# Copies inside SBUF of the keys' and the queries' parts issued from GpSimd's queue instead of SyncE's, in a one-core S5 and sliding-window attention layer

## The chip, the cores and the metric

The kernel runs on one core of a Trainium2 chip. The metric is the device time of one execution in microseconds (us), from the program's start on the core to its end. The engines are named as the profile names them: TensorE (PE, with its weight loads as PEld), VectorE (DVE), ScalarE (ACT), GpSimd (POOL) and SyncE (SP). A DMA is issued by an instruction on the queue of one of SyncE, ScalarE and GpSimd, and that queue is worked off in order.

## What is computed

One layer on x of 1024 tokens by 1024 features, in float32: a projection into six parts, an S5 state-space branch over `u`, sliding-window attention of 8 query heads on 2 key heads over blocks of 128 tokens, both gated by a SiLU, an output projection, and a gate with a per-layer embedding. Cut to what matters here:

```python
hn = rms_norm(h, pre_norm_g[i])
u_ssm, z_ssm, q, k, v, z_attn = jnp.split(hn @ w_in[i], SPLIT_IDX, axis=-1)
ssm_out = s5_branch(u_ssm, ...) * jax.nn.silu(z_ssm)      # scan, gelu, then a Glu with w_glu
attn_out = swa_branch(q, k, v, attn_sinks[i]) * jax.nn.silu(z_attn)
mixed = jnp.concatenate([ssm_out, attn_out], axis=-1) @ w_out[i]
h = h + rms_norm(mixed, post_norm_g[i])
gate = jax.nn.sigmoid(h @ pl_w_gate[i] + pl_b_gate[i])
h = h + gate * (p[i] @ pl_w_proj[i])

# in swa_branch, for each block of 128 queries and the two blocks of keys that it sees:
scores = jnp.einsum('bnqkgd,bnskd->bnkgqs', qb, kb) * scale   # plus ALiBi bias, masked
m = jnp.maximum(jnp.max(scores, axis=-1, keepdims=True), sink)
e = jnp.exp(scores - m)
probs = e / (jnp.sum(e, axis=-1, keepdims=True) + jnp.exp(sink - m))
```

## The kernel before

**Large matmuls.** Each float32 operand is split into a high part and a remainder (`split_to`: ScalarE rounds to the high part on L88, VectorE subtracts on L89), and `product` makes three matmuls of each: high by high (L116), remainder by high (L118), high by remainder (L120). The weights come in parts of 256 KB: `load_part` loads one into `w_st` (L94, on SyncE's queue) and splits it into `w_hi` and `w_lo`. There are two `w_st`, so a load must wait until both parts of the one before last are made, and four of each `w_hi` and `w_lo`.

**State-space branch.** It runs in eight batches of four channel groups. `into_states` of a batch loads `U` and `coef` (L500), builds `mt`, which TensorE transposes (L515), forms the batch's inputs (`w`), and stores a small table `t7` to DRAM (L537) and reads it back in another layout as `tz` (L539); `phases` makes `co` and `si` on VectorE; `scan` runs the recurrence (L579) and swaps halves by two DMAs (L568, L569); `outputs` multiplies with `tz` and `qt` into `ps_y` (L592, L594), applies the gelu on ScalarE (L596, with a load of its function table) and stores `y` to DRAM (L599).

**Projections between the batches.** `project_k` stands ahead of the batches. The list `tiles` (values, four tiles of queries, four of `z_attn`, two of `z_ssm`) is dealt out over the batches, so that TensorE has these matmuls to do while VectorE works on the scan. The code of a batch has a raised priority.

**Keys.** `project_k` scales the keys into `k_f` (128 rows: two key heads of 64 features) and splits them into `k_hi` and `k_lo`. For the scores each head's 64 rows must stand in both halves of the partitions: eight DMAs of 64 rows by 1024 float32 (256 KB each) copy `k_hi` and `k_lo` into `kk` (L616, L617).

**Queries and attention.** `queries(b)` splits a block's 128 queries into `bq_hi` and `bq_lo`, of which there is one buffer each, and four DMAs of 64 by 512 float32 (128 KB each) put the high part of a key head's queries and their remainder into the two halves of `bq` (L710, L711). A unit is half a block (four heads), sixteen in all, whose steps are interleaved with other work: `scores` (GpSimd copies the sink into `sc`, L731; TensorE multiplies `bq` with `kk`, L737 and L738; in block 0 ScalarE copies the scores to `sc`, L740), `maxima` (GpSimd masks in block 0, L748; VectorE, L754), exponents on ScalarE (L761), the reciprocal (L766) and the normalisation on ScalarE or VectorE (L769, L771), transposes (L776), the copy to `p` (L778), values (L794).

**Glu.** It loads `w_glu` (L858) and, for a chunk of channels, the batches' `y` from DRAM into `y_all` (L886), multiplies them in float32 (L866) and gates with a tanh (L869). Its first tiles run between the first units of the attention. The output projection and the tail with the per-layer embedding follow.

**What sets the order.** The program's text gives priorities; a scheduler with a simulated timeline then orders the instructions of each engine's queue, DMA issues among them, and puts in the waits. So an edit in one place can move instructions on any engine after it.

Of the kernel before, what the change touches and what calls it, by code (L numbers as in the profile page):

```python
# [11 lines left out]
F32 = mybir.dt.float32  # L12
# [41 lines left out]
def layer_kernel(  # L54
# [3 lines left out]
    nc = tc.nc  # L58
    V, S, Q, PE = nc.vector, nc.scalar, nc.gpsimd, nc.tensor

    with ExitStack() as top:
# [16 lines left out]
        def t4(shape, dt, name):  # L78
            return mp.tile(shape, dt, name=name, tag="t4", bufs=BUFS["t4"])

        def t2(shape, dt, name, tag):
            return mp.tile(shape, dt, name=name, tag=tag, bufs=BUFS[tag])
# [4 lines left out]
        def split_to(hi, lo, t):  # L87
            S.activation(hi, t, AF.Copy)  # L88
            V.tensor_tensor(out=lo, in0=t, in1=hi.bitcast(F32), op=ALU.subtract)  # L89
# [82 lines left out]
        def place(k):  # L172
            return (x_st if k < 4 else x_sq)[:, k % 4, :]
# [97 lines left out]
        def project(m):  # L271
            w = load_split(w_in[m], KT)
            ps = psum_pair()
            product(ps, w, xact, [(k, k) for k in range(KT)])
            return ps
# [190 lines left out]
        with tc.issue_after(loaded.ins):  # L466
            nc.sync.dma_start(out=t7_dr[:, :, :, 0:CH, :].rearrange("c g q k n -> (g q) c (k n)"),
                                in_=zero.unsqueeze(1).broadcast_to([GB * PC, G // GB, CH * PC]))
# [78 lines left out]
        def phases(b):  # L547
            gs = slice(b["c"] * GB, (b["c"] + 1) * GB)
            co, si = b["co"], b["si"] = big("co", "co"), big("si", "si")

            def a_(t):
                return t[:, gs, :].unsqueeze(3).broadcast_to([P, GB, 8, 16])

            def b_(t):
                return t[:, gs, :].unsqueeze(2).broadcast_to([P, GB, 8, 16])

            a = big("t3", "ta")
            tt(ev(a), a_(e1[1]), b_(e0[1]), ALU.mult)
            tt(ev(co), a_(e1[0]), b_(e0[0]), ALU.mult)
            tt(co, co, a, ALU.subtract)  # L560
            a = big("t4", "ta")
            tt(ev(a), a_(e1[0]), b_(e0[1]), ALU.mult)
            tt(ev(si), a_(e1[1]), b_(e0[0]), ALU.mult)
            tt(si, si, a, ALU.add)
# [7 lines left out]
        def scan(b):  # L572
            w, w2, co, si, c = (b[n] for n in ("w", "w2", "co", "si", "c"))
            tt(w2, w2, si, ALU.mult)
            tt(w, w, co, ALU.mult)
            tt(w, w, w2, ALU.add)
            s = b["s"] = big("s", "w")
            for g in range(GB):
                V.tensor_tensor_scan(out=s[:, g * NC : (g + 1) * NC],  # L579
                                     data0=r8[:, c * GB + g : c * GB + g + 1].broadcast_to([P, NC]),  # L580
                                     data1=w[:, g * NC : (g + 1) * NC], initial=0.0, op0=ALU.mult, op1=ALU.add)
            b["s2"] = swapped(s, nc.sync)

        def outputs(b):
            s, s2, co, si, c, U, tz, qt = (b[n] for n in ("s", "s2", "co", "si", "c", "U", "tz", "qt"))
            tt(s2, s2, si, ALU.mult)
            tt(s, s, co, ALU.mult)
            tt(s, s, s2, ALU.subtract)
            y = t2([P, GB, NC], F32, "y", "sw")
            ps = bank("y")  # L590
            for g in range(GB):
                PE.matmul(ps[:, g * NC : (g + 1) * NC], lhsT=tz[:, g * P : (g + 1) * P], rhs=U[:, g, :],  # L592
                          start=True, stop=False)
                PE.matmul(ps[:, g * NC + 1 : (g + 1) * NC], lhsT=qt[:, g * P : (g + 1) * P],  # L594
                          rhs=s[:, g * NC : (g + 1) * NC - 1], start=False, stop=True)
            S.activation(y, ps.rearrange("p (g c) -> p g c", c=NC), AF.Gelu_apprx_tanh)  # L596
            for g in range(GB):
                r = (c % 2) * 64 + g * PC
                nc.sync.dma_start(out=y_dr[c // 2][r : r + PC].rearrange("q i c -> i q c"), in_=y[:, g, :])  # L599


        def scaled(ps, t, scale=1.0):
            for h, o in enumerate(ps):
                hs = slice(h * HALF, (h + 1) * HALF)
                V.scalar_tensor_tensor(out=t[:, hs], in0=o, scalar=scale, in1=rstd[:, hs], op0=ALU.mult, op1=ALU.mult)
            return t

        def project_k():
            t = scaled(project(8), t4([P, T], F32, "k_f"))
            lo = t4([P, T], F32R, "k_lo")  # L610
            hi = t4([P, T], F32R, "k_hi")
            split_to(hi, lo, t)
            for kv in range(2):
                for half in range(2):
                    rows = slice(64 * half, 64 * half + 64)
                    nc.sync.dma_start(out=kk_hi[rows, kv, :].bitcast(F32), in_=hi[64 * kv : 64 * kv + 64].bitcast(F32))  # L616
                    nc.sync.dma_start(out=kk_lo[rows, kv, :].bitcast(F32), in_=lo[64 * kv : 64 * kv + 64].bitcast(F32))  # L617

        def project_v():
            vt = scaled(project(9), t4([P, T], F32, "v_f"))  # L620
# [33 lines left out]
        kk_hi, kk_lo = kk[:, 0], kk[:, 1]  # L654
# [8 lines left out]
        with tc.high_priority(offset=AHEAD):  # L663
            into_states(batch[0])
            phases(batch[0])
        project_k()
        tiles = ([project_v] + [partial(project_q, m) for m in range(4)] + [partial(project_z_attn, m) for m in range(4)]
                 + [partial(project_z_ssm, m) for m in range(2)])
        for c, b in enumerate(batch):
            with tc.high_priority(offset=AHEAD):  # L670
                scan(b)
                if c + 1 < len(batch):
                    phases(batch[c + 1])
                outputs(b)
                if c + 1 < len(batch):
                    into_states(batch[c + 1])
            for f in tiles[len(tiles) * c // len(batch) : len(tiles) * (c + 1) // len(batch)]:
                f()

# [19 lines left out]
        def queries(b):  # L701

            qs = slice(b * P, (b + 1) * P)
            hi = t2([P, 4, P], F32R, "bq_hi", "mt")
            lo = t2([P, 4, P], F32R, "bq_lo", "m")
            split_to(hi, lo, q_f[:, :, qs])
            st = [t2([P, 4, P], F32R, "bq", t) for t in ("u", "si")]
            for kv in range(2):
                rows, other = slice(64 * kv, 64 * kv + 64), slice(64 - 64 * kv, 128 - 64 * kv)
                nc.sync.dma_start(out=st[kv][rows].bitcast(F32), in_=hi[rows].bitcast(F32))  # L710
                nc.sync.dma_start(out=st[kv][other].bitcast(F32), in_=lo[rows].bitcast(F32))  # L711
            return st

        def stat(name):
# [224 lines left out]
        run_pieces(n, ahead)  # L939
        n = ahead  # L940
        bq = {0: queries(0)}
        for t in range(4 * len(units) + steps[0][1]):
            for step, lag in steps:
# [187 lines left out]
```

## Time and profile before

| | |
|---|---|
| median of 3 runs | 534.99 us (534.62 to 535.94) |
| the profiled execution | 535.14 us |
| its span in the trace | 533.4 us |
| TensorE busy | 97% of the span |
| VectorE | 71% |
| ScalarE | 40% |
| GpSimd | 2% |
| granted TensorE clock, mean | 0.992 of full speed |
| chain that ended last | PE 80%, DVE 9%, DMA 7%, SyncE's queue 1% |

The profiled execution is 0.15 us above the median of the runs, and its span is 1.74 us shorter than its own time, which holds what lies around the program. "Busy" counts instructions and not issues of DMAs. The chain is followed back from the last instruction to what released it; a share of it is what a faster step could at most give.

### The profile page before, as it was taken

To read this page: it belongs to the slowest core of one execution; us is meant where nothing else is said; L and a number is where in the kernel's file an instruction comes from. 1 tells how busy PE (TensorE), PEld (TensorE's weight loads), DVE (VectorE), ACT (ScalarE), POOL (GpSimd) and SP (SyncE) were. 2 spreads that over 40 slices of the span, in tenths; PEclk is the share of its full clock that TensorE was granted. 3 is DMA by queue.
4 is the path that set the end of the run, shared out by engine and by line. 5 is a ranking of instruction groups with operands and counts; after the bars stand their busy time and mean duration, and the time that the engine had idled before them with its cause. 6 is when DMAs were issued, how large, how long until landed. Compare 5 with 4: busy or idle time off the path is not lost.

```text
span 533.4 us, 7319 instructions
## 1 busy us (share of the span) xinstructions
PE 517.3 (97%) x2472; PEld 410.4 (77%) x2472; DVE 379.8 (71%) x864; ACT 214.2 (40%) x443; POOL 8.6 (2%) x37
## 2 busy tenths in 40 slices
PE   7999999999999999999899999999999998999996
PEld 5888887888888888886445767777788886888886
DVE  4778997989889898654699667666467679736232
ACT  5676120311122322233775656667332373223121
POOL 1000000000000000010000000000000000000000
PEclk9999999899999999999999999999999989999999
DMA  7961638344443434559575122101111165124112
GB/s 268 372 233 60 217 93 196 95 128 121 122 117 97 120 95 117 176 145 252 169 213 190 47 60 60 30 22 39 61 49 30 67 218 174 65 80 172 66 39 79
DMA packets 48053, 66.10 MB, mean 124 GB/s; under 512 B 10128, under 2 KB 25232, under 8 KB 48016
## 3 DMA queue, kind: packets, MB, share of 16 engines
q1 hardware_dynamic: 46736, 63.54, 38.6%
q10 hardware_dynamic: 1280, 2.10, 1.5%
q8 instruction: 19, 0.31, 0.3%
q14 instruction: 18, 0.15, 0.1%
HBM read 44.12 MB, written 11.01 MB: 103 GB/s over the span
## 4 chain that ended last, share of the span: by engine, by line
PE 80%; DVE 9%; DMA 7%; SPq 1%; issue 1%; ACT 1%; ACTq 0%; DVEq 0%
PE ps_mm L118 18%; PE ps_mm L116 18%; PE ps_mm L120 18%; PE ps_tab L120 4%; PE ps_tab L116 4%; PE ps_tab L118 4%; PE ps_mm L866 3%; DMA y_all<-y_dr 2%; PE ps_w L794 2%; PE ps_y L794 2%; PE ps_tab L737 1%; PE ps_tab L738 1%; PE ps_y L594 1%; PE ps_w L520 1%; DVE e L314 1%
## 5 line engine op out<-in xcount | busy, mean ns | idle before, releaser
L88 ACT ACTIVATE w_hi<-w_st 128x512 fp32r<-128x512 f32 (+1 forms) x68 | 41.2, 606 | 132.3 <-PE ps_mm L118 80.6
L116 PE MATMUL ps_mm<-x_hi,w_hi 128*128 128x512 f32 x272 | 86.3, 399 | 2.3 <-ACT x_hi L178 1.7
L118 PE MATMUL ps_mm<-x_lo,w_hi 128*128 128x512 f32 x272 | 87.7, 399 | 0.0
L120 PE MATMUL ps_mm<-x_hi,w_lo 128*128 128x512 f32 x272 | 87.4, 398 | 0.0
L89 DVE TENSOR_TENSOR w_lo<-w_st,w_hi 128x512 fp32r<-128x512 f32 (+1 forms) x68 | 44.8, 659 | 38.7 <-ACT w_hi L88 32.4
L116 PEld LDWEIGHTS ps_mm<-x_hi,w_hi 128*128 128x128 f32 x272 | 51.3, 191 | 13.6 <-ACT x_hi L178 2.2
L118 PEld LDWEIGHTS ps_mm<-x_lo,w_hi 128*128 128x128 f32 x272 | 51.6, 191 | 10.5
L120 PEld LDWEIGHTS ps_mm<-x_hi,w_lo 128*128 128x128 f32 x272 | 51.2, 191 | 10.2 <-DVE w_lo L89 0.3
L118 PE MATMUL ps_mm<-h_lo,w_hi 128*128 128x512 f32 (+1 forms) x96 | 30.8, 380 | 0.0
L116 PE MATMUL ps_mm<-h_hi,w_hi 128*128 128x512 f32 (+1 forms) x96 | 30.8, 380 | 0.0
L120 PE MATMUL ps_mm<-h_hi,w_lo 128*128 128x512 f32 (+1 forms) x96 | 30.7, 380 | 0.0
L761 ACT ACTIVATE sc<-sc,mx 128x129 f32<-128x129 f32 x64 | 25.1, 395 | 12.9 <-DVE mx L754 12.7
L866 PE MATMUL ps_mm<-y_all,w_glu 128*128 128x512 f32 x64 | 29.1, 596 | 1.2 <-DMA w_glu<-in_w_glu 1.2
L1028 DVE SCALAR_TENSOR_TENSOR o_t<-o_t,pls 128x512 f32<-128x512 f32 (+1 forms) x17 | 10.9, 658 | 20.0 <-ACT o_t L1027 20.0
L866 PEld LDWEIGHTS ps_mm<-y_all,w_glu 128*128 128x128 f32 x64 | 11.5, 190 | 13.5 <-issue 10.6
L116 PE MATMUL ps_mm<-m_hi,w_hi 128*128 128x512 f32 x64 | 21.8, 404 | 0.0
L120 PE MATMUL ps_mm<-m_hi,w_lo 128*128 128x512 f32 x64 | 21.7, 402 | 0.0
L118 PE MATMUL ps_mm<-m_lo,w_hi 128*128 128x512 f32 x64 | 21.7, 398 | 0.0
L118 PEld LDWEIGHTS ps_mm<-h_lo,w_hi 128*128 128x128 f32 x96 | 18.0, 188 | 3.5
L116 PEld LDWEIGHTS ps_mm<-h_hi,w_hi 128*128 128x128 f32 x96 | 18.0, 188 | 3.5
L120 PEld LDWEIGHTS ps_mm<-h_hi,w_lo 128*128 128x128 f32 x96 | 18.0, 188 | 3.5
L314 DVE TENSOR_TENSOR sw<-sw,si 128x512 f32<-128x512 f32 x16 | 11.1, 693 | 11.4 <-DMA sw<-s 8.4
(265 smaller groups left out, 1022.9 us busy)
## 6 DMA issues: line engine op xcount, KB each, us to landing
w_st<-in_w_in SPq DMA_DIRECT2D x30, 256.0 KB
w_st<-in_w_out SPq DMA_DIRECT2D x16, 256.0 KB
w_st<-in_w_gate SPq DMA_DIRECT2D x16, 256.0 KB
x<-in_xT SPq DMA_DIRECT2D x8, 512.0 KB
out_T<-o_t SPq DMA_DIRECT2D x15, 256.0 KB
x_sq<-in_xT SPq DMA_DIRECT2D x4, 512.0 KB
x_st<-in_x SPq DMA_DIRECT2D x4, 512.0 KB
x_sq<-in_x SPq DMA_DIRECT2D x4, 512.0 KB
```

What stands on the lines that cost most here:

```text
L88: S.activation(hi, t, AF.Copy)
L89: V.tensor_tensor(out=lo, in0=t, in1=hi.bitcast(F32), op=ALU.subtract)
L116: PE.matmul(o, lhsT=wh, rhs=ah(ka, h), start=f, stop=False)
L118: PE.matmul(o, lhsT=wh, rhs=al(ka, h), start=False, stop=False)
L120: PE.matmul(o, lhsT=wl, rhs=ah(ka, h), start=False, stop=l)
L314: V.tensor_tensor(out=o, in0=a, in1=b, op=op)
L520: PE.matmul(ps[:, g * NC : (g + 1) * NC], lhsT=m[:, g * P : (g + 1) * P], rhs=U[:, g, :], start=True, stop=True)
L594: PE.matmul(ps[:, g * NC + 1 : (g + 1) * NC], lhsT=qt[:, g * P : (g + 1) * P], rhs=s[:, g * NC : (g + 1) * NC - 1], start=False, stop=True)
L761: S.activation(self.sc[:, m, :], self.sc[:, m, :], AF.Exp, bias=self.mx[:, m : m + 1], scale=-1.0, accum_out=self.sm[:, m : m + 1])
L794: PE.matmul(pv[64 * kv : 64 * kv + 64], lhsT=v[:, cols], rhs=p[:, 2 * kv : 2 * kv + 2, :], start=n == 0, stop=n == len(parts) - 1)
L866: PE.matmul(self.ps, lhsT=self.w[:, k, :], rhs=glu_in["y"][:, self.hf, k, :], start=k == 0, stop=k == 3)
L1028: V.scalar_tensor_tensor(out=t, in0=t, scalar=1.0, in1=pls[2 * m + h][:, a : a + n], op0=ALU.add, op1=ALU.mult)
```

## The change

The eight copies of the keys and the four per block of the queries are issued by `nc.gpsimd` instead of `nc.sync`. `project_k` no longer issues the keys' copies itself: it returns four functions, of two copies each, and the loop over the batches calls one of them at the end of each of the first four batches. Line numbers behind it grow by two (the queries' copies are L712 and L713 now, the keys' L615 and L616).

```diff
             split_to(hi, lo, t)
-            for kv in range(2):
-                for half in range(2):
-                    rows = slice(64 * half, 64 * half + 64)
-                    nc.sync.dma_start(out=kk_hi[rows, kv, :].bitcast(F32), in_=hi[64 * kv : 64 * kv + 64].bitcast(F32))
-                    nc.sync.dma_start(out=kk_lo[rows, kv, :].bitcast(F32), in_=lo[64 * kv : 64 * kv + 64].bitcast(F32))
+            def place(kv, half):
+                rows = slice(64 * half, 64 * half + 64)
+                nc.gpsimd.dma_start(out=kk_hi[rows, kv, :].bitcast(F32), in_=hi[64 * kv : 64 * kv + 64].bitcast(F32))
+                nc.gpsimd.dma_start(out=kk_lo[rows, kv, :].bitcast(F32), in_=lo[64 * kv : 64 * kv + 64].bitcast(F32))
+            return [partial(place, kv, half) for kv in range(2) for half in range(2)]
...
-        project_k()
+        placed = project_k()
...
             for f in tiles[len(tiles) * c // len(batch) : len(tiles) * (c + 1) // len(batch)]:
                 f()
+            if placed:
+                placed.pop(0)()
...
             for kv in range(2):
                 rows, other = slice(64 * kv, 64 * kv + 64), slice(64 - 64 * kv, 128 - 64 * kv)
-                nc.sync.dma_start(out=st[kv][rows].bitcast(F32), in_=hi[rows].bitcast(F32))
-                nc.sync.dma_start(out=st[kv][other].bitcast(F32), in_=lo[rows].bitcast(F32))
+                nc.gpsimd.dma_start(out=st[kv][rows].bitcast(F32), in_=hi[rows].bitcast(F32))
+                nc.gpsimd.dma_start(out=st[kv][other].bitcast(F32), in_=lo[rows].bitcast(F32))
             return st
```

SyncE's queue around the keys, before (`t_dr` is the table `t7` in DRAM, `w_st` the staged weights of the next projection):

```order
L94 DMA w_st<-in_w_in 128x512 x2
L537 DMA t_dr<-t_713 16x8x16 x4
L539 DMA tz<-t_dr 128x1x128 x4
L616 DMA kk<-k_hi 64x1024
L617 DMA kk<-k_lo 64x1024
```

Three more pairs like the last two follow, and then `coef` and the weights. The same place now:

```order
L94 DMA w_st<-in_w_in 128x512 x2
L537 DMA t_dr<-t_713 16x8x16 x4
L539 DMA tz<-t_dr 128x1x128 x4
L500 DMA coef<-in_bc 128x256
L94 DMA w_st<-in_w_in 128x512 x3
L568 DMA sw<-s 64x512
L569 DMA sw<-s 64x512
```

The eight rows of the keys are gone, and `coef` and three loads of weights stand right behind `tz`.

GpSimd's queue from the keys to the first unit of the attention, now; before, it held the same rows without the DMAs:

```order
L701 AFFINE_SELECT own_t<-own_t 128x128
L615 DMA kk<-k_hi 64x1024 x4
L616 DMA kk<-k_lo 64x1024 x4
L689 IOTA dist 128x128
L690 IOTA near 128x128
L712 DMA bq<-bq_hi 64x512
L713 DMA bq<-bq_lo 64x512
L712 DMA bq<-bq_hi 64x512
L713 DMA bq<-bq_lo 64x512
L733 COPY sc<-sink 128x4
L750 AFFINE_SELECT sc<-sc 128x4x128
```

All eight copies of the keys stand in one piece, behind masks made at the start (`own_t`); the queries' copies stand ahead of the units' copies of the sink.

ScalarE's queue between the exponents of the first unit and the second block's queries, before:

```order
L761 ACT_TABLE_LOAD
L761 ACTIVATE sc,sm<-sc,mx 128x129 x4
L88 ACTIVATE bq_hi<-q_f 128x512
L596 ACT_TABLE_LOAD
L596 ACTIVATE y<-ps_y 128x512
L740 COPY sc<-ps_tab 128x2x128 x2
L778 COPY p<-ps_w 128x512
L839 ACTIVATE z_tanh<-z_half 128x1024
```

and now:

```order
L763 ACT_TABLE_LOAD
L763 ACTIVATE sc,sm<-sc,mx 128x129 x4
L596 ACT_TABLE_LOAD
L596 ACTIVATE y<-ps_y 128x512
L742 COPY sc<-ps_tab 128x2x128 x2
L780 COPY p<-ps_w 128x512
L88 ACTIVATE bq_hi<-q_f 128x512
L841 ACTIVATE z_tanh<-z_half 128x1024
```

`bq_hi` has moved behind the gelu `y` of the last batch, the scores' copies and `p`.

## Rows read from the trace of the kernel before

**Rows 1.** The page, busy time of each engine: us, share of the span, instructions.

```profile
PE 517.3 (97%) x2472; PEld 410.4 (77%) x2472; DVE 379.8 (71%) x864; ACT 214.2 (40%) x443; POOL 8.6 (2%) x37
```

**Rows 2.** Waits of TensorE, whole span: what waited, for what, us in total, times, longest us.

```profile
PE ps_tab L515 <- DVE mt L314: 1.7, 1, 1.7
...
PE ps_y L776 <- ACT sc L769: 1.4, 1, 1.4
PE ps_mm L866 <- DMA w_glu<-in_w_glu: 1.2, 2, 0.7
...
PE ps_tab L737 <- ACT sc L740: 1.1, 1, 1.1
```

**Rows 3.** Stretches: us, busy PE, PEld, DVE, ACT, POOL, clock, DMA share, GB/s.

```profile
82.00:84.00 2.00, 2.00 (x10) 1.66 (x9) 2.00 (x5) 0.00 (x0) 0.00 (x0) 1.00 1.01 205
...
94.00:96.00 2.00, 1.96 (x14) 1.89 (x15) 2.00 (x6) 0.59 (x1) 0.00 (x0) 0.80 0.36 131
96.00:98.00 2.00, 2.00 (x6) 1.61 (x5) 2.00 (x4) 0.00 (x0) 0.00 (x0) 0.50 0.56 131
98.00:100.00 2.00, 2.00 (x9) 1.56 (x9) 2.00 (x5) 0.00 (x0) 0.00 (x0) 0.84 0.02 3
246.00:248.00 2.00, 2.00 (x10) 1.39 (x9) 0.00 (x0) 0.00 (x0) 0.54 (x3) 1.00 1.05 213
```

**Rows 4.** The chain of waits through 74 to 96 us: start us, us, what.

```profile
87.98 3.88 DMA w_st<-in_w_in
...
91.94 0.64 ACT w_hi L88
```

**Rows 5.** VectorE's timeline: start us, us, instruction, count, [idle before it <- its end].

```profile
80.07 0.73 DVE L89 TENSOR_TENSOR w_lo<-w_st,w_hi 128x512 fp32r<-128x512 f32 x1
...
92.60 0.69 DVE L89 TENSOR_TENSOR w_lo<-w_st,w_hi 128x512 fp32r<-128x512 f32 x1 [3.38 <-ACT w_hi L88]
```

**Rows 6.** SyncE's timeline, 74 to 94 us, issues of DMAs.

```profile
74.87 3.17 SPq L539 DMA_DIRECT2D tz<-t_dr  x4
78.09 0.60 SPq L616 DMA_DIRECT2D kk<-k_hi  x1
...
85.43 1.21 SPq L617 DMA_DIRECT2D kk<-k_lo  x1
86.75 1.13 SPq L500 DMA_DIRECT2D coef<-in_bc  x1
87.98 5.67 SPq L94 DMA_DIRECT2D w_st<-in_w_in  x3
```

**Rows 7.** ScalarE's timeline, 241 to 262 us.

```profile
250.50 0.63 ACT L88 ACTIVATE bq_hi<-q_f 128x512 fp32r<-128x512 f32 x1 [9.05 <-DMA bq<-bq_hi]
...
252.44 0.60 ACT L596 ACTIVATE y<-ps_y 128x512 f32<-128x512 f32 x1
```

**Rows 8.** SyncE's timeline, 236 to 270 us.

```profile
241.98 0.47 SPq L710 DMA_DIRECT2D bq<-bq_hi  x1
...
245.00 2.32 SPq L886 DMA_DIRECT2D y_all<-y_dr  x3
```

**Rows 9.** The chain of waits through 238 to 272 us.

```profile
239.95 5.72 DMA y_all<-y_dr
...
256.57 2.35 DMA bq<-bq_lo
```

**Rows 10.** TensorE's timeline: the first use of `tz`, the last matmul of a batch.

```profile
77.68 0.39 PE L592 MATMUL ps_y<-U,tz 128*128 128x128 f32 x2
...
245.61 0.39 PE L594 MATMUL ps_y<-s,qt 128*128 128x127 f32 x2
```

**Rows 11.** The tile `kk`, its first matmuls: ns min, median, max; first and last start.

```profile
L737 PE MATMUL ps_tab<-kk,bq x64: 222/281/682, 234.8 to 355.6; 128*128 128x256 f32 x56, 128*128 128x128 f32 x8
```

**Rows 12.** A stretch, columns as in rows 3.

```profile
280.00:420.00 140.00, 140.00 (x679) 104.02 (x678) 91.80 (x244) 75.57 (x208) 2.03 (x9) 1.00 0.19 57
```

**Rows 13.** GpSimd's groups of instructions: count, busy us, mean ns, idle before and releasers.

```profile
L731 POOL COPY sc<-sink 128x4 f32<-128x4 f32 x16 | 4.8, 300 | 121.6 <-PE ps_y L776 42.7 <-DVE s L579 30.3 <-PE ps_w L776 30.2
```

## The prediction

> **What bounds the kernel now.** The page comes first. TensorE is busy 517.3 us of the 533.4 us span [rows 1], so a change that touches no matmul can win only where TensorE stands idle or runs at its lower clock, at most 16 us and a little. The wait table of TensorE then says where that is [rows 2]; the reader is to see that four of its waits have to do with work beside which the changed copies stand: 1.7 us before the transposes of `mt`, 1.1 and 1.4 us behind ScalarE's `sc`, and 1.2 us for `w_glu`. They lie in two places.
>
> *Place 1, 92 to 99 us.* TensorE waits 1.7 us for VectorE's `mt`. Behind that wait the granted clock drops: 0.80, 0.50 and 0.84 of full speed in three stretches of 2 us [rows 3]; 0.50 is the 1.2 GHz level. The missing share is (0.20 + 0.50 + 0.16) x 2 us = 1.72 us. The chain of waits [rows 4] says why `mt` is late: VectorE stood idle 3.38 us ahead of a `w_lo` [rows 5], which waited for ScalarE's `w_hi`, which waited for a weight load of 3.88 us that SyncE issued only at 87.98. SyncE's own rows [rows 6] show what it did before: behind the copies of `tz` it issued the eight copies of the keys, from 78.09 to 86.64, and then `coef` and the weights. A timeline lists no semaphore for the weight load, but its buffer is free when VectorE's `w_lo` at 80.07 has read it, by 80.80 [rows 5]. So it was late only because it stood in line behind the keys.
>
> *Place 2, 246 to 270 us.* ScalarE idled 9.05 us before `bq_hi` at 250.50, and that wait names the copies of `bq` as its end [rows 7]: `bq_hi` has one buffer, and the copies that read it had to finish. Those copies were issued at 241.98 and later between two groups of `y_all` loads [rows 8], one of which took 5.72 us, while a later copy of `bq` took 2.35 us [rows 9]. The gelu `y` of the next batch stands behind `bq_hi` on ScalarE and came at 252.44 [rows 7], though its last matmul began at 245.61 [rows 10]. The scores' `sc` copies, the storing of `y` and the third load of `y_all` follow from it. TensorE's idle time here sums to 1.1 + 1.4 + 1.2 = 3.7 us [rows 2].
>
> **The change, part by part.** The keys' eight copies leave SyncE's queue. By the order they are not spread: nothing ahead of the eight on GpSimd's queue has to wait for anything late, so they go out one after another as soon as `k_hi` and `k_lo` exist. The keys are first read at 234.8 us [rows 11], so how long they take costs nothing in itself.
>
> 1. *Weights of place 1.* Without the 8.55 us of issuing, `coef` and the weights follow `tz` at 78.04; the buffer lets the weights go at 80.8, 7.2 us earlier. VectorE comes to its `w_lo` at 92.60 - 3.38 = 89.22. Even a load of 5.72 us, the longest in these rows, ends at 86.5. VectorE's 3.38 us and TensorE's 1.7 us of idle time go: **-1.7 us**. With no idle time ahead of it the clock has no cause to fall: **-1.72 us**; it was at 1.00 in the stretches before [rows 3].
>
> 2. *Keys against `tz`.* Now the copies of the keys run from some 73 us on and meet the storing of `t7` and the load of `tz`, which had the DMA engines nearly to themselves. TensorE reads the first `tz` at 77.68 without having waited [rows 10], and that `tz` was issued at 74.87 [rows 6], so its latency may be at most 2.81 us. An uncontended copy took 2.35 us, a load on full engines 5.72 us [rows 9]. The cost lies between 0 and 5.72 - 2.81 = 2.9 us; I take **+0.9 us**, near the lower third, since the keys' first copies start only as `t7` is stored, and the engines' share is at 1.01 from 82 to 84 us, when five or six of them were issued [rows 3].
>
> 3. *Queries in place 2.* In the new order ScalarE does the gelu `y`, the `sc` copies and `p` ahead of `bq_hi`, and the copies of `bq` neither wait behind the `y_all` loads on SyncE nor delay them. `y` can then go at about 246.1 instead of 252.44. What is late next is not that: the third tile of `w_glu` still stands behind six `y_all` loads, and the engines were at 1.05 of their share from 246 to 248 [rows 3]. Bounds: nothing gained (0), all of it gained (-3.7). I leave a wait of 1.3 us for `w_glu` and `y_all`, about what `w_glu` costs today, and take **-2.3 us**.
>
> 4. *Queries in the attention blocks.* From 280 to 420 us TensorE is busy 140.00 of 140.00 us [rows 12], so there is nothing to gain. GpSimd gets four copies per block, in order with its copies of `sc`, of 0.30 us each [rows 13]. No row shows a copy issued from GpSimd; issues on SyncE held it 0.47 us (`bq`) to 1.21 us (a copy of the keys) [rows 6, 8], and I take 1.1 us, near the dearer of the two, since no row excludes more; what more would cost is rival D. A block takes (355.6 - 234.8) / 7.5 = 16.1 us [rows 11] and GpSimd would be busy 4 x 1.1 + 2 x 0.3 = 5 us of it: **0**. Its cover is those 11 us.
>
> 5. *SyncE without the 32 issues of `bq`*, of some 0.5 us: outside the two places the path doesn't go through it, since TensorE doesn't wait there: 0.
>
> The sum is -1.7 - 1.72 + 0.9 - 2.3 = -4.82 us. The profiled execution took 535.14 us, 0.15 above the median of the runs, so the forecast is 535.14 - 4.82 = 530.32, **530.3 us**. Its own range goes from 535.14 - 1.7 - 1.72 - 3.7 = 528.0 (all of place 2, nothing for `tz`) to 535.14 - 1.7 - 1.72 + 0.9 = 532.6 us (place 1 alone). Smaller than 0.3% (1.6 us) a difference from the median can't be told from none.
>
> **The rivals.**
>
> *A. Place 2 is bound by the transfers, not by the queue.* The engines stand at 1.05 of their share at its start [rows 3]; moving an issue from one queue to another moves no byte less. For it: the two `y_all` loads are what the chain goes through. Against it: ScalarE's 9.05 us is a wait for an order of work, and that order changes. Then only place 1 is won: 535.14 - 3.42 + 0.9 = 532.6 us. The Trainium skill ("DMA: Bandwidth & Descriptors", "Issuing engines are not separate DMA queues") says just this, that DMAs from any engine run on the same 16 engines and a second issuer saves only the sequencer's time. The trace agrees for place 1, where it is the sequencer's 8.55 us that go, and leaves place 2 open. Chance 0.14.
>
> *B. The keys take the engines from `tz`*, and TensorE waits the full 2.9 us at 77.68, after which its clock falls as it did behind 1.7 us in place 1 (another 1.72 us). Place 1 is given back: -3.42 + 2.9 + 1.72 = +1.2, and place 2 stands: 535.14 + 1.2 - 2.3 = 534.0 us. Against it: half of the keys' copies need `k_lo`, which VectorE makes after `k_hi`, and a few us of overlap must more than double a latency. Chance 0.08.
>
> *C. GpSimd can't issue while VectorE works.* VectorE is busy 2.00 of every 2.00 us in place 1's run-up [rows 3]. If GpSimd were shut out, the keys would wait till VectorE idles and only then go; they are not needed for 140 us, `tz` is not disturbed (+0), place 1 is still won. The copies of `bq` would each lose some us, which takes place 2's gain: 535.14 - 3.42 = 531.7 us. The Trainium skill ("SBUF — State Buffer", "SBUF: two separate sides") tells of such a shut-out: a copy issued from GpSimd that takes some 620 ns alone took 3100 ns beside a VectorE copy in its two-port mode. No run here shows it yet; the same page's "Who interferes with whom" holds two-input operations, which fill VectorE here, to bother only GpSimd's reads. Chance 0.08.
>
> *D. GpSimd's queue becomes the bound of the attention (slower).* Its queue is in order, and its `sc` copies stand behind the copies of `bq`; VectorE's maxima and all that follows wait for `sc`. The point from which it decides: a copy of `bq` holds GpSimd over (16.1 - 0.6) / 4 = 3.9 us, by its issue or by waiting for `bq_hi`'s buffer. At 4.5 us a block grows by 2.5 us, and seven blocks by 17: 530.3 + 17 = 547 us. For it: GpSimd does 4.8 us of such `sc` copies in the whole kernel [rows 13] and issues nothing, so no row shows that it can keep up, and each copy waits for its buffers in line. Against it: the issues of SyncE are a quarter as long. Chance 0.14.
>
> **The change does not do what it says:** "spread over later tiles" does not hold in the order (all eight stand together). It costs nothing where the keys are concerned, since the queue that mattered was SyncE's; it is the cause of term 2.
>
> **How the numbers follow.** Forecast 0.56, A 0.14, B 0.08, C 0.08, D 0.14. The range is 527.9 to 534.3: it takes the forecast's own, A, B and C, and leaves out D and the tails. Faster by over 0.3% (below 533.4): forecast, C and nearly all of A, 0.56 + 0.08 + 0.12 = 0.76. Within: B and the rest of A, 0.10. Slower: D, 0.14.
>
> **What would show it.** In the profile after: SyncE issues the weights near 80.8 us right behind `coef`; no idle time ahead of the transposes of `mt`; granted clock 1.00 between 92 and 100 us. If TensorE waits at its first `tz`, term 2 is right in kind, and its length is the price. In place 2 ScalarE's `y` comes before `bq_hi`, near 246 us, and the wait for `bq` is gone; the remaining waits of TensorE there sum to about 1.3 us. GpSimd's rows give the price of an issue, 1.1 us by me; VectorE waiting for GpSimd's `sc` in every block would be D. I am wrong if TensorE's total idle time falls by less than 1.5 us, or if a new wait of over 1 us appears anywhere outside the two places.

## The result, and the profile after

The change makes the kernel slower: 544.20 us median of 5 runs (543.45 to 545.11) against 535.94 (534.62 to 536.54), a ratio of 1.0147 with an interval of 1.0120 to 1.0174. The forecast was 530.3 us with a range up to 534.3.

The page after, busy time, and then the waits of TensorE over the whole span:

```profile
PE 520.3 (96%) x2472; PEld 411.4 (76%) x2472; DVE 379.6 (70%) x864; ACT 214.0 (39%) x443; POOL 29.3 (5%) x77
```

```profile
PE ps_y L592 <- DMA tz<-t_dr: 7.5, 1, 7.5
PE ps_tab L116 <- ACT w L88: 2.1, 1, 2.1
...
PE ps_mm L868 <- DMA w_glu<-in_w_glu: 1.6, 1, 1.6
PE ps_mm L116 <- ACT a_hi L88: 1.2, 1, 1.2
```

Of the four waits of [rows 2] three are gone (for `mt`, and both behind `sc`), and the one for `w_glu` is 1.6 us. In their place stands one of 7.5 us, for `tz`. It is the rival B of the prediction, much larger than it was priced. GpSimd's timeline, SyncE's, and the chain of waits show how it came about:

```profile
72.09 2.19 POOL L615 DMA_DIRECT2D kk<-k_hi  x4 [69.40 <-ACT k_hi L88]
74.27 2.02 POOL L616 DMA_DIRECT2D kk<-k_lo  x4
```

```profile
71.97 4.10 SPq L537 DMA_DIRECT2D t_dr<-t  x4
76.11 7.41 SPq L539 DMA_DIRECT2D tz<-t_dr  x4
83.62 0.54 SPq L500 DMA_DIRECT2D coef<-in_bc  x1
84.58 11.80 SPq L94 DMA_DIRECT2D w_st<-in_w_in  x3
```

```profile
74.33 1.74 SPq L537
...
76.11 9.07 DMA tz<-t_dr
...
85.23 0.79 PE ps_y L592 x2
```

GpSimd issued all eight copies, 2.1 MB, in 4.2 us. SyncE had needed 8.55 us for them [rows 6]. The storing of `t7` and the load of `tz` were issued into the same stretch. SyncE's four issues of `tz` took 7.41 us, where they had taken 3.17 [rows 6]; the first `tz` took 9.07 us, where it had taken 2.81 at most, and landed at 85.18. Stretches of 2 us (columns as in rows 3) show full DMA engines, TensorE without work, and the lower clock behind the wait:

```profile
72.00:74.00 2.00, 2.00 (x13) 1.70 (x12) 2.00 (x6) 0.00 (x0) 1.91 (x4) 1.00 0.60 172
...
76.00:78.00 2.00, 1.73 (x8) 1.11 (x6) 2.00 (x5) 0.08 (x1) 0.29 (x1) 1.00 1.03 264
78.00:80.00 2.00, 0.00 (x0) 0.00 (x0) 1.08 (x2) 0.00 (x0) 0.00 (x0) 1.00 1.00 276
...
86.00:88.00 2.00, 2.00 (x7) 1.52 (x6) 1.19 (x3) 0.63 (x1) 0.00 (x0) 0.50 0.47 129
88.00:90.00 2.00, 2.00 (x6) 1.60 (x5) 2.00 (x4) 0.00 (x0) 0.00 (x0) 0.50 0.00 0
```

A measure of place 1 that all kernels share is the time from TensorE's first forming of batch inputs (L520) to its second. Before:

```profile
71.76 1.05 PE L520 MATMUL ps_w<-U,m 128*128 128x128 f32 x8
...
101.10 1.05 PE L520 MATMUL ps_w<-U,m 128*128 128x128 f32 x8
```

and after:

```profile
71.43 1.05 PE L520 MATMUL ps_w<-U,m 128*128 128x128 f32 x8
...
107.86 1.05 PE L520 MATMUL ps_w<-U,m 128*128 128x128 f32 x8
```

That is 29.34 us before and 36.43 us after, so +7.1 us, most of the 8.3 us between the medians. The spans of the two profiles differ by 9.4 us (533.4 and 542.8). Besides these 7.1 us, 2.7 lie behind the last such forming: from there to the end it takes 322.1 us before and 324.8 after.

A second loss is seen only in the groups of instructions. TensorE's matmuls of the values, in the kernel before (columns: line, operation, shapes, count, busy us, mean ns, idle before) and after:

```profile
L794 PE MATMUL ps_w<-p_own,v_step 128*64 128x256 f32 x28 | 7.5, 392 | 0.0
L794 PE MATMUL ps_y<-p,v_f 128*64 128x256 f32 x32 | 6.5, 405 | 0.0
L794 PE MATMUL ps_w<-p,v_f 128*64 128x256 f32 x32 | 5.2, 404 | 0.0
L794 PE MATMUL ps_y<-p_own,v_step 128*64 128x256 f32 x28 | 5.0, 386 | 0.0
```

```profile
L796 PE MATMUL ps_w<-p_own,v_step 128*64 128x256 f32 x28 | 7.6, 395 | 0.0
L796 PE MATMUL ps_y<-p,v_f 128*64 128x256 f32 x32 | 6.5, 405 | 0.0
L796 PE MATMUL ps_w<-p,v_f 128*64 128x256 f32 x32 | 6.5, 404 | 0.0
L796 PE MATMUL ps_y<-p_own,v_step 128*64 128x256 f32 x28 | 6.3, 390 | 0.0
```

The same 120 records, of nearly the same length each, fill 26.9 us of TensorE's time instead of 24.2. (One matmul of the program is two records here, so these are 60 matmuls.)

### The profile page after: what moved, and what is told of

It reads as the page before. It is cut to its first block, busy times and chain, and to the rows that moved or that the text cites. A ratio compares the mean times of both kernels' runs of the same rounds, so it can differ in the third digit from the quotient of the medians.

```text
span 542.8 us, 7350 instructions
## 1 busy us (share of the span) xinstructions
PE 520.3 (96%) x2472; PEld 411.4 (76%) x2472; DVE 379.6 (70%) x864; ACT 214.0 (39%) x443; POOL 29.3 (5%) x77
## 4 chain that ended last, share of the span: by engine, by line
PE 84%; DVE 6%; DMA 5%; SPq 2%; issue 1%; ACT 1%; ACTq 0%; DVEq 0%
PE ps_mm L116 18%; PE ps_mm L118 18%; PE ps_mm L120 18%; PE ps_mm L868 4%; PE ps_tab L120 4%; PE ps_tab L116 4%; PE ps_tab L118 3%; PE ps_w L796 2%; PE ps_y L796 2%; DMA w_glu<-in_w_glu 2%; DMA tz<-t_dr 2%; PE ps_tab L739 2%; PE ps_tab L740 1%; PE ps_y L592 1%; PE ps_w L520 1%; PE ps_y L594 1%
## 5 line engine op out<-in xcount | busy, mean ns | idle before, releaser
L116 PE MATMUL ps_mm<-h_hi,w_hi 128*128 128x512 f32 (+1 forms) x96 | 31.6, 390 | 0.0
L118 PE MATMUL ps_mm<-m_lo,w_hi 128*128 128x512 f32 x64 | 20.6, 393 | 0.0
```

What stands on the lines that cost most here:

```text
L116: PE.matmul(o, lhsT=wh, rhs=ah(ka, h), start=f, stop=False)
L118: PE.matmul(o, lhsT=wh, rhs=al(ka, h), start=False, stop=False)
```

## The experiments

All kernels of one group ran on one chip, with the kernel before beside them; its median was 536.2 to 537.5 us there, so ratios are compared and not times. Orders are those of the built kernels.

### The two halves of the change, half the bytes, and a real spread

e1 is the kernel before with the queries' copies issued by `nc.gpsimd`; e2 is the change with the queries' copies put back on `nc.sync`.

> Keys back on SyncE as before the change, only the queries' copies on GpSimd. Theory V (the keys' 2.1 MB, all issued at 72 to 76 us, fill the DMA engines ahead of the storing of t7 and the load of tz, and that costs the 7.5 us wait; the queries' copies are harmless or a small gain): no wait for tz, place 1 as in the kernel before (1.7 us idle, clock to 0.5), place 2 about 2 us better; 532.5 to 535 us, 1 to 3 us below the kernel before. Rival Q (the queries' copies on GpSimd cost time in the attention): slower than before by 1 us or more.

> Only the keys' copies on GpSimd, the queries' back on SyncE. Theory V: the whole loss is here: TensorE waits 7 to 8 us for tz at about 77 us, its clock falls behind the wait, 542 to 546 us. Rival Q: 536 to 538 us.

e3 splits the keys' copies by columns:

```diff
-            return [partial(place, kv, half) for kv in range(2) for half in range(2)]
+            for kv in range(2):
+                for half in range(2):
+                    place(kv, half, slice(0, HALF))
+            return [partial(place, kv, half, slice(HALF, T)) for kv in range(2) for half in range(2)]
...
-            if placed:
-                placed.pop(0)()
+            if c == 1:
+                gate = Q.tensor_copy(out=held, in_=b["tz"][:, GB * P - 1 : GB * P])
+                with tc.issue_after(gate.ins):
+                    for f in placed:
+                        f()
```

> As the change, but of each key copy only the first half of the columns goes at once (eight copies of 128 KB); the other eight halves are held on GpSimd's queue behind a small copy that reads batch 1's tz. Theory V: the bytes ahead of tz halve, so the wait for tz falls from 7.5 to 2 to 4.5 us, and the time to 537 to 541 us. Rival P (the number of copies issued from GpSimd, or its way of issuing, is what holds the others up, not the bytes): the wait stays at 6 to 8 us and the time at 543 or more.

e4 holds each pair of copies behind a small GpSimd copy that can't start before a batch's `tz` is there:

```diff
             if placed:
-                placed.pop(0)()
+                gate = Q.tensor_copy(out=held[:, c : c + 1], in_=b["tz"][:, GB * P - 1 : GB * P])
+                with tc.issue_after(gate.ins):
+                    placed.pop(0)()
```

> As the change, but the four pairs of key copies are really spread: GpSimd issues a pair only after a small copy that reads the tz of batch 0, 1, 2, 3. Theory V: no wait for tz, SyncE free, so no wait for mt and no fall of the clock near 92 us; with place 2's 2 us, 530.5 to 533.5 us, below both kernels. Rival P (GpSimd's issuing disturbs whenever it happens): waits for tz or weights move to other batches, and the time stays above 536 us.

Measured: e1 1.0054 (1.0030 to 1.0077), e2 1.0089 (1.0064 to 1.0114), e3 1.0035 (1.0005 to 1.0064), e4 0.9948 (0.9922 to 0.9974). The waits for `tz`, of e2 and of e3:

```profile
PE ps_y L592 <- DMA tz<-t_dr: 8.0, 1, 8.0
```

```profile
PE ps_y L592 <- DMA tz<-t_dr: 2.9, 1, 2.9
```

The wait goes with the bytes ahead of `tz` and not with the number of copies: 2.1 MB 7.5 and 8.0 us, 1.05 MB by the same eight copies 2.9 us, none in e4. That carries theory V as far as the keys go. In e4, GpSimd's timeline and TensorE's show the real spread:

```profile
80.05 1.91 POOL L681 COPY held<-tz 128x1 f32<-128x1 f32 x1 [77.36 <-DMA tz<-t_dr]
81.89 0.67 POOL L615 DMA_DIRECT2D kk<-k_hi  x1
...
103.26 0.68 POOL L681 COPY held<-tz 128x1 f32<-128x1 f32 x1 [20.18 <-DMA tz<-t_dr]
```

```profile
76.40 0.39 PE L592 MATMUL ps_y<-U,tz 128*128 128x128 f32 x2
...
90.95 0.60 PE L515 MATMUL ps_tab<-ident,mt 128*128 128x128 f32 x4
```

From the first forming to the second it is 70.48 to 96.41, so 25.93 us: 3.41 us less than before, where term 1 of the prediction had -3.42. But e1 contradicts V's second half: the queries alone are not harmless, they cost 0.5%. The two halves add up to the whole (0.54% and 0.89% against 1.47%).

### Who issues, when, and the queries' half

e5 is e4 with the queries' copies on `nc.sync`; TensorE's order is then the same as in the kernel before, row by row. e7 is e2 with the keys' copies on `nc.scalar`. e8 is e5 with all eight copies behind the first gate. e9 is e4 with the queries' copies on `nc.scalar`.

> Keys on GpSimd, held one pair each behind the tz of batches 0 to 3, and the queries' copies back on SyncE; TensorE's order is then that of the kernel before. Theory V+O (the keys' bytes ahead of tz are one half of the loss; the other is the queries' part, by which the scheduler puts the last attention units later, 2 to 3.5 us behind the first Glu product for the output projection): place 1 takes 25.9 us from the first to the second forming of the batch inputs on TensorE (29.3 before), the stretch from the output projection's first matmul to the end as before (246 to 248 us), in all 2.5 to 4.5 us below the kernel before, and below the held keys with the queries on GpSimd. Rival G (the queries on GpSimd gain, as forecast for place 2): slower than that kernel by some 2 us.

> Keys issued at once as in the change, but from ScalarE's queue; the queries on SyncE. Theory V (bytes on the DMA engines, whoever issues them): TensorE waits 4 to 9 us for tz or what follows from it near 77 us, and the time is 4 to 9 us above the kernel before. Rival P (copies from GpSimd are what holds the others up): no wait for tz over 1 us, time within 2 us of the kernel before.

> Keys on GpSimd, all eight behind the tz of batch 0 alone; the queries on SyncE. Theory V: what counts is only to be behind tz: TensorE has no wait for tz, place 1 takes 26 to 27.5 us, 1.5 to 4 us below the kernel before. Rival S (2.1 MB in one piece is too much wherever it is put, so that spreading is needed): weights or coef come late near 85 to 92 us and TensorE waits again over 1.5 us there; within 1 us of the kernel before.

> Keys held as in the first kernel here, the queries' copies issued from ScalarE. Its order, too, puts the last attention unit behind the output projection's first matmuls of the attention half. Theory V+O: the end costs as much as with the queries on GpSimd, 248.5 to 251 us from the output projection's first matmul to the end, so the time lies 1 to 3 us above the held keys with the queries on SyncE. Rival Q (GpSimd's copies themselves cost the time at the end): 246 to 248 us there.

Measured: e5 0.9940 (0.9912 to 0.9969), e7 0.9913 (0.9877 to 0.9949), e8 1.0006 (0.9983 to 1.0030), e9 0.9955 (0.9927 to 0.9982).

e5 has place 1 at 25.9 us, as expected. The stretch to the end was 249.7 us and not 246 to 248, 3.4 us of it lost to a lower clock in two falls; and against e4 (0.9948, another chip) the intervals overlap: the pair shows no cost of the queries on GpSimd, but has room for one of up to some 0.5%, so it does not settle the queries' half.

e7 is a plain miss of V as I had put it: the keys went at once from another queue, the wait for `tz` was 0.6 us, as rival P had it, and the kernel became faster. ScalarE's queue and the chain show why:

```profile
71.55 1.15 ACTq L615 DMA_DIRECT2D kk<-k_hi  x2
73.62 1.67 ACTq L616 DMA_DIRECT2D kk<-k_lo  x2
...
75.61 1.11 ACTq L615 DMA_DIRECT2D kk<-k_hi  x1
...
78.89 0.61 ACTq L616 DMA_DIRECT2D kk<-k_lo  x1
...
80.23 0.47 ACTq L615 DMA_DIRECT2D kk<-k_hi  x1
81.30 0.47 ACTq L616 DMA_DIRECT2D kk<-k_lo  x1
```

```profile
76.23 4.98 DMA tz<-t_dr
```

The eight copies are not "at once" there: they are spread over 10 us between ScalarE's own work, and three of them come behind the first load of `tz`, which took 4.98 us. That is more than the 2.81 at most of the kernel before and less than the 9.07 of the change, so copies from ScalarE's queue delay `tz` too. Besides, the scheduler put the first matmul with `tz` later: its turn came at 80.64, and it waited 0.62 us, to 81.26. At the place of before, near 77.7, the same `tz` would have cost some 3.5 us (an estimate from these rows). So two things had been mixed, how late `tz` is and where its reader stands in TensorE's queue; e10 takes them apart. No run issues all eight copies within some 4 us from another queue, so whether GpSimd's copies hold up `tz` more than the same bytes at the same pace from elsewhere stays open.

e8 shows that behind `tz` in one piece is not enough. Place 1 is at 25.9 us, but from the second forming to the third it takes 98.33 to 115.35, 17.0 us where the kernel before takes 12.5, with two waits behind VectorE (1.1 and 1.4 us) and a fall of the clock there. That is rival S's mechanism, though what comes late is not what it named.

e9's stretch to the end was 248.4 us, between what the two theories had expected, so it told nothing by that measure. What it was worth came later: its values' matmuls take 22.1 us.

### The place in TensorE's queue, the order of the attention's end, and SyncE alone

e10 is e2 with one instruction moved, the first matmul that reads `tz`, which is queued behind a matmul of the next projection:

```diff
+                if c == 1:
+                    tc.add_manual_dep(batch[0]["first"].ins, third[n_f + 9].ins.name,
+                                      mybir.DependencyInfo(mybir.DependencyClass.NoSync, mybir.DependencyReason.DATA), reason="later")
```

> Keys at once on GpSimd as in the change, the queries on SyncE; of all instructions only the first matmul that reads tz is moved, about 8 us later on TensorE's queue. Theory W (the copies make tz land some 8 us later, at 85 us; that costs only because the matmul that waits for it stands at the head of TensorE's in-order queue while other matmuls are ready behind it): the wait for tz falls from 8.0 us to under 1 us, the clock stays at 1.00 there, and the time drops by 5 us or more against the keys alone, to 0 to 4 us below the kernel before. Rival L (VectorE, too, is held up by late transfers, or the next weights are late): TensorE waits 3 us or more for mt or for weights near 90 us instead, and the time stays above the kernel before.

e11 is e5 with one number changed:

```diff
-        n, ahead, end = min(pieces), 10, max(pieces) + 1
+        n, ahead, end = min(pieces), 12, max(pieces) + 1
```

> Keys held on GpSimd, queries on SyncE, but the attention starts two pieces of filling work later (the start value of ahead is 12 instead of 10), which puts the last unit's values behind the first matmuls of the attention half of the output projection, as in the change, without any queries' copy on GpSimd. Theory O (the queries' part costs by the order at the attention's end): TensorE waits about 1.2 us for a_hi, and from the last forming of a batch's inputs to the end it takes 323 to 325.5 us without what a lower clock costs (320.3 before; 322.7 for the same kernel with ahead 10); 1 to 3 us above that kernel. Rival Q (GpSimd's copying itself): no wait for a_hi, and 320 to 322.5 us there.

e12 is e7 with the queries' copies on `nc.gpsimd`.

> Keys issued at once from ScalarE (5 us below the kernel before with the queries on SyncE) and the queries on GpSimd, with the order of the change behind the keys. Theory O: the same stretch costs 2 to 3.5 us more than with the queries on SyncE, so 1.5 to 3.5 us below the kernel before. Rival N (the queries' part costs nothing here): 4 to 6 us below it.

e13 keeps every copy on `nc.sync` and queues the keys' behind a later load of weights (`loads` collects `load_part`'s DMAs):

```diff
-            if placed:
-                placed.pop(0)()
+            if c == 2:
+                with tc.issue_after(loads[-1].ins):
+                    for f in placed:
+                        f()
```

> Keys and queries stay on SyncE; the keys' copies only stand later in its queue, behind the loads of the weights that were late. Theory: leaving SyncE was not needed, only giving way: no wait for mt near 92 us, 25.9 to 27 us between the first two formings of batch inputs (29.3 before), 2 to 4 us below the kernel before. Rival T (the copies meet the next batch's t7 and tz at 104 us there): TensorE waits over 1.5 us for tz or mt near 104 to 112 us, within 1 us of the kernel before.

Measured: e10 1.0059 (1.0035 to 1.0083), e11 0.9927 (0.9901 to 0.9953), e12 0.9959 (0.9932 to 0.9985), e13 0.9999 (0.9970 to 1.0028).

In e10 the wait for `tz` is gone altogether, and yet most of the loss stays: rival L's mechanism. The waits of TensorE, VectorE's timeline and the chain:

```profile
PE ps_tab L517 <- DVE mt L316: 2.5, 1, 2.5
```

```profile
83.89 0.23 DVE L316 TENSOR_TENSOR t<-last,ddt 128x64 f32<-128x64 f32 x1 [4.39 <-DMA t_dr<-t]
```

```profile
74.55 9.23 DMA t_dr<-t
```

VectorE can't write the next `t7` before the store of this one has read it, and that store took 9.23 us, landing at 83.78 behind the keys. VectorE stood 4.39 us, `mt` came 2.5 us late, and the clock fell behind that wait. So the keys' bytes held up the store of `t7` as much as the load of `tz`, and reached TensorE over either: mending one path shows the other.

In e11 the last unit's values stand as late as in the change, but TensorE does not wait for `a_hi`, and the stretch from the last forming to the end takes 325.5 us, 322.1 without the 3.4 us lost to the clock. Theory O fell. e12 against e7 (0.9959 and 0.9913, two chips) has the sign of a cost of the queries on GpSimd, though the intervals overlap, and its values' matmuls take 26.9 us again.

e13 is equal to the kernel before. Place 1 is at 25.9 us, but the copies then meet the next batch's loads, as rival T had it, though the wait is for `U` and not for `tz` or `mt`: 1.97 us, to 111.44.

### What the queries' half costs

By then the values' matmuls took 26.9 us in each of the five kernels with the queries on GpSimd (the change, e1, e3, e4, e12), 24.1 or 24.2 us in those with them on SyncE, and 22.1 in e9, while the count of value matmuls that stand single in TensorE's order, apart from their like, is 24, 16 and 10. (A single one is two records of the trace; two that stand together are four.) A stretch of TensorE's timeline before shows both kinds:

```profile
346.79 0.65 PE L794 MATMUL ps_y<-p,v_f 128*64 128x256 f32 x4
347.27 0.60 PE L794 MATMUL ps_y<-p_own,v_step 128*64 128x256 f32 x4
...
351.93 0.65 PE L794 MATMUL ps_w<-p,v_f 128*64 128x256 f32 x4
352.51 0.44 PE L776 MATMUL ps_y<-ident,sc 128*128 128x128 f32 x2
352.88 0.65 PE L794 MATMUL ps_w<-p_own,v_step 128*64 128x256 f32 x2
353.46 0.33 PE L776 MATMUL ps_y<-ident,sc 128*128 128x128 f32 x1
353.71 0.65 PE L794 MATMUL ps_w<-p_own,v_step 128*64 128x256 f32 x2
```

Unbroken, the second four records take 0.60 us; broken by a transpose, each two of them take 0.65 us, so a matmul alone takes as long as two together. The last group forbids the breaks: a unit's transposes are queued behind the last values' matmul of the unit before. The edit is the same in the change (e16), the kernel before (e17), e12 (e14) and e7 (e15):

```diff
-                for m in range(4):
-                    PE.transpose(pt[:, m * P : (m + 1) * P], self.sc[:, m, 0:P], ident)
+                i = units.index(self)
+                with ExitStack() as apart:
+                    if i:
+                        apart.enter_context(tc.issue_after(units[i - 1].last.ins))
+                    for m in range(4):
+                        PE.transpose(pt[:, m * P : (m + 1) * P], self.sc[:, m, 0:P], ident)
...
-                        PE.matmul(pv[64 * kv : 64 * kv + 64], lhsT=v[:, cols], rhs=p[:, 2 * kv : 2 * kv + 2, :],
+                        self.last = PE.matmul(pv[64 * kv : 64 * kv + 64], lhsT=v[:, cols], rhs=p[:, 2 * kv : 2 * kv + 2, :],
```

> The change as it is, and in addition each unit's transposes may stand on TensorE's queue only behind the values' matmuls of the unit before. Theory I (the queries' part costs 2.6 us because its order breaks more of the values' matmuls apart by transposes; 24 single matmuls of the values in it against 16 before): 8 are left here, so the values' matmuls take about 21.6 us instead of 26.9 and the time falls by 4 to 6 us below the change's, to 536 to 541 us, with place 1's wait for tz of 7 to 8 us still there. Rival R (the single matmuls only look costly; TensorE's time goes elsewhere): the values' sum stays over 25 us, the time within 1.5 us of the change's.

> The kernel before with the same addition; none of the values' matmuls stands single (16 before). Theory I: the values' matmuls take about 19 us instead of 24.2, and the time lies 3 to 6 us below the kernel before, if the last unit, which ends later in this order, brings no wait of its own. Rival R: within 1.5 us of the kernel before.

> Keys at once from ScalarE, queries on GpSimd, and the same addition: 8 single matmuls left of 24. Theory I: values' matmuls at 21 to 22 us, 5 to 8 us below the kernel before. Rival R: 1 to 3 us below it, as without the addition.

> Keys at once from ScalarE, queries on SyncE, and the same addition: no single matmul of the values. Theory I: values' matmuls at about 19 us, 7 to 10 us below the kernel before, the best version here. Rival R: 4 to 5 us below it, as without the addition.

Measured: e16 1.0033 (1.0000 to 1.0067), e17 0.9945 (0.9913 to 0.9977), e14 0.9902 (0.9868 to 0.9936), e15 0.9901 (0.9865 to 0.9937). The values' matmuls take 21.5 us in e16 and e14, 18.8 in e17 and e15. Two of the four groups of e17, with the new wait that the order brings:

```profile
L798 PE MATMUL ps_w<-p,v_f 128*64 128x256 f32 x32 | 5.2, 405 | 1.4 <-DVE p_own L788 1.4
...
L798 PE MATMUL ps_y<-p_own,v_step 128*64 128x256 f32 x28 | 4.2, 379 | 0.0
```

Theory I's sums (21.6 and 19) came out to 0.2 us. Each single matmul costs (26.9 - 24.2) / 8 = 0.34 us of the sum, and (24.2 - 18.8) / 16 is 0.34 as well. The change falls from 1.47% to 0.33% over the kernel before, by 1.1% or some 6 us, with its wait for `tz` (7.1 us) still there. The times follow the sums less well. e17 gains 0.55%, 3 us for 5.4, and e14 against e12 some 3 us for 5.4. e15, of which theory I forecast 7 to 10 us below the kernel before, lies 5.3 us below it, where e7 was without the addition (0.9901 and 0.9913): in e15 rival R's forecast came out, and no gain is shown. In e17 and e15 the new order makes TensorE wait 2.8 us for `p_own` and 1.2 us for `a_hi`, and in e15's profile the granted clock stood at 0.50 behind these waits, from 374 to 380 us; that this is what ate the gain is argued from these rows and not tested. The addition moves other instructions too, so a part of these differences may be theirs. e14, e15 and e7 have the lowest ratios, some 5 us below the kernel before; between them the runs don't decide.

| kernel | keys | queries | ratio to before | L520 first to second, us | wait for tz, us | values, us |
|---|---|---|---|---|---|---|
| before | SyncE | SyncE | 1 | 29.3 | none | 24.2 |
| the change | GpSimd, at once | GpSimd | 1.0147 | 36.4 | 7.5 | 26.9 |
| e1 | SyncE | GpSimd | 1.0054 | 31.6 | none | 26.9 |
| e2 | GpSimd, at once | SyncE | 1.0089 | 35.7 | 8.0 | 24.1 |
| e3 | GpSimd, half at once | GpSimd | 1.0035 | 29.1 | 2.9 | 26.9 |
| e4 | GpSimd, spread | GpSimd | 0.9948 | 25.9 | none | 26.9 |
| e5 | GpSimd, spread | SyncE | 0.9940 | 25.9 | none | 24.2 |
| e7 | ScalarE | SyncE | 0.9913 | 26.8 | 0.6 | 24.2 |
| e10 | GpSimd, at once, reader later | SyncE | 1.0059 | 31.9 | none | 24.2 |
| e15 | ScalarE, no breaks | SyncE | 0.9901 | 26.8 | 0.7 | 18.8 |

## Why the prediction was wrong, point by point

**Term 1 (the weights of place 1) was right.** e4 measures it alone: -3.41 us for -3.42. In the change itself the wait for `mt` is gone too, but the stretch is longer by what follows, and the weights were issued at 84.58 and not near 80.8.

**Term 2 (the keys against `tz`) is the step that failed.** It said "+0.9 us" between 0 and 2.9. Measured was a wait of 7.5 us. Four stretches from 84 to 92 us at clocks of 0.50, 0.50, 0.50 and 0.71 cost about 3.0 us of TensorE's time more (the missing share times its busy time in each). With term 1's gain these make place 1: 7.5 + 3.0 - 3.4 = 7.1 us, as measured. Three things were wrong in it. It bounded the latency of `tz` by the longest that the rows of before showed, 5.72 us, as though a row bounded what other traffic can do; the bytes come nearer: 2.1 MB at the 264 to 276 GB/s of the stretches after are 7.6 to 8 us. (That this is the wait almost to the tenth is partly luck, since other transfers stand in the same stretch and the keys' last copies landed at 84.7.) It took one transfer, while `tz` is the second of a chain of two, behind the store of `t7`, and both stood in the crowd. And it reckoned with the pace of SyncE, 8.55 us for eight copies (at term 4's 1.1 us an issue they take 8.8), where GpSimd needs 4.2. The rule by the Trainium skill that the prediction cites for rival A ("DMA: Bandwidth & Descriptors", "Issuing engines are not separate DMA queues") bears on this: the trace agrees that copies from GpSimd share the engines with SyncE's (share 1.00 to 1.03, and `tz` at 9.07 us). The prediction used it against the gain of place 2 and not for the price of place 1.

**Rival B was the right mechanism at the wrong price.** It put place 1 at +1.2 us net; measured +7.1. e3 (half the bytes) and e4 (none) show that the keys' bytes ahead of `tz` are the cause. e10 shows that more than the wait at `tz` hung on it.

**Term 3 (place 2) was right about the idle time and wrong about the rest.** TensorE's idle time there fell from 3.7 us to the 1.6 of `w_glu`, with 1.3 forecast, and by the forecast mechanism: the gelu `y` came 0.4 us behind the start of its last matmul (252.78 and 252.35), where before it came 6.8 us behind. So rival A, by which nothing could be won there, does not hold. But the step read the gain from the stretch alone, while the new order went on to the end of the attention: 8 more single matmuls of the values (2.7 us) and 1.2 us of wait for `a_hi`. With the 2.1 us won that is +1.8 us, of the 2.7 that the change loses behind the last forming. So the queries' half, forecast at -2.3 us, costs 0.54% by itself (e1). That the breaks are a cause is shown by e16, whose interval lies below the change's; whether the rest of e1's loss is the longer fall of the clock in its place 1 (31.6 us where before has 29.3) is not settled.

**Term 4 and rivals C and D.** An issue on GpSimd took 0.52 us, not 1.1, as the two groups of `bq` copies show. (SyncE's issues of the keys, from which the 1.1 was taken, ran to 1.44 us and not only to 1.21.)

```profile
L712 POOL DMA_DIRECT2D bq<-bq_hi x16 | 8.3, 521 | 51.8 <-PE ps_tab L740 15.8 <-ACT w_hi L88 12.9 <-ACT m_hi L88 7.5
L713 POOL DMA_DIRECT2D bq<-bq_lo x16 | 8.3, 519 | 0.0
```

D did not occur. Nor did C: from 72 to 74 us VectorE was busy 2.00 of 2.00 us and GpSimd issued for 1.91 of them.

**The order told that the copies are not spread, and I priced that at nothing but term 2.** The edit says "later tiles", but a place in the program's text is only a priority: here all eight copies went as soon as `k_hi` and `k_lo` were made. e4 had to add a real dependency to hold them.

**The signs that it named of being wrong came.** TensorE's idle time rose, from 16.1 us (533.4 - 517.3) to 22.5 (542.8 - 520.3), and new waits of over 1 us stand outside the two places, for `tz` and for `a_hi`.

## What to carry to other kernels

A slow issuing queue may be what paces a large transfer that nobody waits for: before taking it off, count its bytes against the engines' rate and ask which short, dependent transfers will stand in the same stretch. To move a ready transfer later, give it something to wait for; a later line of the program did not do it here. And when a scheduler reorders an engine that is never idle, compare the busy time of its groups and not only its waits: here the same matmuls cost 24.2 or 26.9 us by what stood between them.

## What the runs showed of the hardware

- The pace of issue depends on the queue: the same eight 256 KB copies took 4.2 us to issue from GpSimd (0.51 to 0.66 us each), 8.55 from SyncE, and some 10 from ScalarE, which had other work between. From GpSimd or from ScalarE, they held up a load on SyncE's queue: the first `tz` took 9.07 us in the change, 4.98 in e7 and 2.81 at most in the kernel before.
- Beside a VectorE that was full of two-input operations GpSimd's issues stayed at 0.51 to 0.52 us but for the first, of 0.66. A GpSimd copy did not stay so even: the 128x1 copies of the gate in e4 took 0.20 to 1.91 us, the longest while VectorE was busy 2.00 of 2.00 us. The Trainium skill ("SBUF — State Buffer", "Who interferes with whom") says that two-input operations contend with a GpSimd instruction that reads SBUF; the trace fits that, and no run here tells it from another cause.
- A value matmul that stands apart from its like takes 0.34 us more of TensorE's busy sum than one of two that stand together, with the same mean of 379 to 405 ns a record; only the busy sum of the group shows it. Why is not settled.
- Whether a wait of 1 to 2 us is followed by a fall of the granted clock differs between kernels: behind the wait for `w` near 443 us the clock stayed at 1.00 in the kernel before (1.5 us, then 1.1 us more at 445) and fell to 0.50 in the change (2.1 us, to 450, then 1.1 us more). This fall, at 0.75, 0.50 and 0.90 in three stretches of 2 us from 452 on, cost some 1.7 us, so single profiles can differ by that much.
